# A hybrid encoder block on one Trainium2 core: two Strassen products with the low halves first, one load order for gate values and weights, a row of reciprocals, and another split of the last adds

## The chip, the cores and the metric

The kernel runs on one core of one Trainium2 chip. A core has five engines that each work through their own instruction list in order: PE (TensorE, matrix products), DVE (VectorE) and ACT (ScalarE) for elementwise work, POOL (GpSimd), and SP (SyncE), which here only issues transfers. They wait for each other by semaphores. The metric is the device time of one execution in microseconds (us); the kernel before takes 2518.39 us (median of 3 runs, 2517.55 to 2518.57).

## The reference, cut to what matters

One residual layer over 512 tokens of width 2048, in float32 (x, weights and output):

```
u  = RMSNorm(x)
q, k, v, conv_a, conv_b, gate_a, gate_b = split(u @ W_in)
y_A = neighbourhood_attention(q, k, v) @ W_attn_o          # 1024 -> 2048
y_B = silu(layer_norm(depthwise_conv(conv_a * sigmoid(conv_b)))) @ W_conv_o   # 1024 -> 2048
h  = x + RMSNorm((sigmoid(gate_a) * y_A + sigmoid(gate_b) * y_B) @ W_out)
u  = RMSNorm(h)
gate, up = split(u @ W_gate_up)                            # 2048 -> 2 x 5632
out = h + RMSNorm((silu(gate) * up) @ W_down)              # 5632 -> 2048
```

## The kernel before, in words

All activations are kept transposed: a tile has 128 channels by 512 tokens. Products are in a two-part form: each float32 operand is cast to a rounded "hi" (ACT, `whi_...`, `...h`) and a remainder "lo" (DVE, `wlo_...`, `...l`), and hi and lo products are added in PSUM. A function `gemm` (L168) does this for a chunk of weights of 128x1024: `wchunk` loads the raw chunk over SP's queue (L134; five buffers `raw`), casts hi on ACT (L135) and subtracts lo on DVE (L136), and for each of eight 128-blocks PE does three matmuls of 512 columns: hi weights by lo activations (L182), hi by hi (L185), lo by hi (L186).

**Strassen pairs.** Most of the two gate projections, of the feed-forward and of the down projection are done two output tiles at a time by a seven-product scheme, `strassen` (L237): 14 pairs g2 to g15, 39 pairs f5 to f43 and 16 pairs d0_0 to d1_14. The operands on the activation side hold hi in the first 256 columns and lo in the last 256. Each `product` (L275) is eight matmuls of 512 columns with the hi weights (L279) and then eight of 256 columns with the lo weights (L281), all into one PSUM tile. The seven are called in the order 11, T2, T1, T3, 21, 22, T4; in the first pair of a run of pairs ("apart": g2, f5, d0_0, d1_0) the 21 comes second. Between them DVE adds one PSUM tile into the next (L305, L310), ACT copies (L272, L287), and the hi and lo parts of the next weight sums are made (L245, L247).

**The merge.** `gated(i, j, ...)` (L724) makes output tile i of W_attn_o (j = 0) or W_conv_o (j = 1): it loads the stored gate value tile `gg` (`load_in_order`, that is a load on SP whose place in the program is kept), does the `gemm` into a PSUM tile `py`, and multiplies on DVE (L729). Sixteen tiles with j = 0 come first; the last operand tiles for them (`ya3` to `ya7`) are split inside the first of them, while three (`YA_EARLY`) are split earlier, in the last gate pair. At tiles 5, 6 and 7 a step of `layer_norm` (L685) is run: the mean by a matmul (`pmu`), eight subtractions (L698) and squares (ACT L381, added on DVE L384); then the column sums `rc_s` on PE (L339), `rc_v` on DVE (L347) and a power on POOL; then `rc_b` on PE (L356), eight multiplications (DVE L706), eight silu (ACT L708) and the hi/lo split `ych`, `ycl` (L713, L714). Then sixteen tiles with j = 1 follow; after each, POOL adds the j = 0 tile (L740) and the sum is split into `mh` on ACT and `ml` on DVE (L145) for W_out.

**Rows of the feed-forward.** The activations of W_down are scaled per token before, and unscaled after, by a row: `rstd` (L333) makes r = v^-1/2 by token with v the mean square, `by_column` (L352) spreads it by four transposing matmuls into a 128x512 row, which ACT copies to SBUF as `row[0]`, `row[1]`. `scaled` (L881, POOL L885) multiplies by it. Later the row is replaced by v * r, its reciprocal, by a second `by_column` and copy, at pair f39 (`ia0`) and between the two runs of d pairs (`ia1`); POOL multiplies results `ys` by it (L1020).

**The end.** The last norm gives `r_b`. Sixteen half tiles are then left in four groups `yg` of 128x1024: DVE multiplies each by the row (L1152); the first `G_ADD` = 2 groups are added to the output in memory by a transfer that accumulates (L1154, issued by POOL); for the others DVE adds the residual `hb` in two halves (L1157), and SP and ACT issue the output transfers (L1161).

**What sets the order.** The Python code is laid out once by a scheduler, which gives every engine a fixed list; `tc.keep_in_program_order` pins an instruction to its place in the program against the other pinned ones. Everything else can be put earlier or later than it is written. At run time each engine keeps to its list and waits where an operand is not there.

Of the kernel before, what the change touches and what calls it, by code (L numbers as in the profile page):

```python
# [25 lines left out]
F32 = mybir.dt.float32  # L26
# [5 lines left out]
P = 128  # L32
# [30 lines left out]
AHEAD = 6  # L63
LEFT, G_ADD = 4, 2
UN_EARLY, YA_EARLY = 2, 3
C_PRE, C_POST, C_FPRE, C_FPOST, C_LNG, C_LNB, C_BDW, C_WDW = 0, 16, 32, 48, 64, 72, 80, 88
# [4 lines left out]
def hybrid_block(ctx: ExitStack, tc, xT, vecs, rpb, mask, w_c0, w_qk, w_v, w_gg, w_cg, w_ao, w_co, w_out, w_g0, w_gu, w_dn, outT):  # L71
# [52 lines left out]

    def wchunk(src, name, parts=1, cast=nc.scalar.copy, raw=None):
        w = src.shape[-1]
        loaded = raw is not None
        raw = raw if loaded else wraw(name)[:, :w]
        hi = wp.tile([P, 1024], F32R, tag="whi", name=f"whi_{name}")[:, :w]
        lo = wp.tile([P, 1024], F32R, tag="wlo", name=f"wlo_{name}")[:, :w]  # L130
        for n in range(parts):
            s = slice(n * w // parts, (n + 1) * w // parts)
            if not loaded:
                nc.sync.dma_start(raw[:, s], src[:, s])  # L134
            cast(hi[:, s], raw[:, s])  # L135
            nc.vector.tensor_tensor(out=lo[:, s], in0=raw[:, s], in1=hi[:, s].bitcast(F32), op=ALU.subtract)  # L136
        taps(rate)
        return hi, lo
# [28 lines left out]

    def gemm(outs, acts, name, n=None, more=None, cols=slice(0, NT), between=(), pin=False, raw=None):  # L168

        n = n or len(acts)  # L170
        between = iter(between)
        for c in range(0, n, 8):
# [3 lines left out]
            for i, (ps, src) in enumerate(outs):  # L176
                hi, lo = wchunk(src[:, c * P : (c + w) * P], f"{name}_{i}_{c}", raw=None if c or i else raw)
                for k in range(w):
                    s = slice(k * P, (k + 1) * P)
                    ah, al = (t[:, cols] for t in acts[c + k])  # L180
                    first, last = c + k == 0, c + k == n - 1
                    mmul = nc.tensor.matmul(ps, hi[:, s], al, start=first, stop=False)  # L182
# [3 lines left out]
                    nc.tensor.matmul(ps, lo[:, s], ah, start=False, stop=last)  # L186
                next(between, lambda: None)()
# [67 lines left out]
    def strassen(w0, w1, op, name, n, s1=None, behind_last=None, first=None, quarters=None, apart=False):  # L255
# [18 lines left out]

        def product(ps, w, b, first=False, last=False):  # L275
            hi, lo = w if isinstance(w, tuple) else halved_weights(w, name)
            ws = [slice(k * P, (k + 1) * P) for k in range(HT)]
            for k, t in enumerate(op[b]):
                nc.tensor.matmul(ps, hi[:, ws[k]], t, start=first and k == 0, stop=False, skip_group_check=True)  # L279
            for k, t in enumerate(op[b]):  # L280
                nc.tensor.matmul(  # L281
                    ps[:, A], lo[:, ws[k]], t[:, A], start=False, stop=last and k == HT - 1, skip_group_check=True
                )

# [22 lines left out]
        s3 = wsum(a11, a21, ALU.subtract, 3)  # L307
        product(y, s3, "T3")
        p5 = copied(z, 3)
# [9 lines left out]
        c11 = done(x, 1)  # L319
        product(z, s4, "22", last=True)  # L320
        c12 = None if behind_last else done(z, 2)
# [9 lines left out]
    def rstd(acc, n, name, blocks=range(NB), pin=False, eps=None):  # L331
# [17 lines left out]
        nc.gpsimd.tensor_tensor(out=r[:, bs], in0=v[:, bs], in1=mhalf[:, bs], op=ALU.pow)  # L349
        return (r, v) if eps else r  # L350

# [372 lines left out]
    def gated(i, j, w, acts, more=None, raw=None):  # L724
        g = slot(f"gg{i}_{j}")
        load_in_order(g, g_d[j * KT + i])
        ps = bank(f"py{i}_{j}")
        gemm([(ps, w[i])], acts, f"y{i}_{j}", n=CT, more=more, raw=raw)
        nc.vector.tensor_tensor(out=g, in0=ps, in1=g, op=ALU.mult)  # L729
        return g  # L730
# [148 lines left out]
    y_d = dr.tile([2, KT, P, NT], F32, name="y_d")  # L879
    inverse = []  # L880

# [40 lines left out]
    for j in range(5, FT):  # L922
# [6 lines left out]
        for n, k0 in enumerate(DN_A):  # L929

            if j == k0 + KT + 1:
                ra, va = rstd([row[n]], KT * P, f"ra{n}", eps=TINY)
                ia = const.tile([P, NB], F32, name=f"ia{n}")
                nc.vector.tensor_tensor(out=ia, in0=va, in1=ra, op=ALU.mult)
                inverse.append(ia)
# [213 lines left out]
    for g, t in enumerate(yg):  # L1149

        out = hb[g] if g < G_ADD else t
        nc.vector.tensor_tensor(out=out, in0=t, in1=rb, op=ALU.mult)  # L1152
        if g < G_ADD:
            nc.gpsimd.dma_start(ov[4 * g : 4 * g + 4, :, B].rearrange("k p t -> p k t"), out, accum_op=ALU.add)  # L1154
            continue
        for m in range(0, 4, 2):
            nc.vector.tensor_tensor(  # L1157
                out=t[:, m : m + 2], in0=t[:, m : m + 2], in1=hb[g][:, m : m + 2], op=ALU.add
            )
# [87 lines left out]
```

## Time and profile before

| what | value |
|---|---|
| median of 3 runs | 2518.39 us (2517.55 to 2518.57) |
| the profiled execution | 2521.2 us, span 2519.4 us |
| granted TensorE clock over the span | 0.996 |
| PE busy | 2493.3 us, 99% of the span, 13399 instructions |
| DVE busy | 2007.7 us, 80% |
| ACT / POOL busy | 1193.5 us (47%) / 456.3 us (18%) |
| transfers | 456.60 MB, mean 181 GB/s |

The span is what lies between the first and the last instruction that the profiler recorded. In rows of the trace the first number is the start in us from the start of the span, the second the duration; "x8" groups eight instructions of one kind that follow each other, with the time from the first start to the last end. Matmuls are pipelined, so that the duration of one is longer than the distance to the next; distances between starts are what counts. What stands in brackets is the idle time of the engine ahead of the row, and what ended it. In windows, "PEclk" is the clock that the throttle granted to TensorE.

By stage: convolution, v and attention up to 500 us; gates 500 to 806; the merge j = 0 from 806 to 894 and j = 1 to 981; W_out to 1158; the feed-forward to 2051; W_down to 2500; the end.

### The profile page before, as it was taken

How to read it: one execution, taken by the hardware profiler on the slowest of the kernel's cores; microseconds unless marked ns; L12 is line 12 of the kernel's file. 1: busy time of each engine (PE TensorE's matmuls, PEld its weight loads, DVE VectorE, ACT ScalarE, POOL GpSimd, SP SyncE). 2: the span in 40 equal slices, each digit the busy share in tenths (PEclk: the TensorE clock that was granted, in tenths of full speed). 3: DMA queues.
4: the chain of work that ended last, by engine and by line, in shares of the span. 5: the costliest groups of instructions: out<-in, count | busy, mean ns of one | idle time of the engine just before them, and what ended most of it. 6: DMA issues, size and time to landing. Idle time of an engine off the chain costs nothing.

```text
span 2519.4 us, 35541 instructions
## 1 busy us (share of the span) xinstructions
PE 2493.3 (99%) x13399; PEld 2156.1 (86%) x13399; DVE 2007.7 (80%) x2566; ACT 1193.5 (47%) x1822; POOL 456.3 (18%) x489
## 2 busy tenths in 40 slices
PE   9999999999999999999999999999999999999997
PEld 7888888888888788889898888888888888888887
DVE  5999897597777555337898888899998889989886
ACT  5223333365555422225455555555555565556453
POOL 0110132220000011001101111122221203632352
PEclk9999999999999999999999999999999999999998
DMA  6246322386667535226455566566666678888886
GB/s 208 93 142 205 104 101 99 134 261 196 183 187 218 187 121 200 95 98 186 145 155 169 171 178 184 174 202 196 203 213 194 214 218 250 242 228 250 222 227 198
DMA packets 160300, 456.60 MB, mean 181 GB/s; under 512 B 17920, under 2 KB 30336, under 8 KB 160128
## 3 DMA queue, kind: packets, MB, share of 16 engines
q1 hardware_dynamic: 109984, 332.70, 38.4%
q0 software_dynamic: 30016, 86.53, 16.6%
q10 hardware_dynamic: 20128, 35.10, 3.7%
q8 instruction: 105, 1.72, 0.3%
q14 instruction: 67, 0.55, 0.1%
HBM read 384.53 MB, written 67.11 MB: 179 GB/s over the span
## 4 chain that ended last, share of the span: by engine, by line
PE 88%; DVE 7%; issue 2%; DMA 1%; ACT 1%; POOL 0%; SPq 0%; DVEq 0%; ACTq 0%; POOLq 0%
PE f L279 20%; PE f L281 10%; PE d L279 8%; PE g L279 7%; PE d L281 4%; PE pd L960 3%; PE g L281 3%; DVE cv L432 3%; PE qk L186 2%; PE qk L185 2%; PE qk L182 2%; PE po L185 2%; PE po L182 2%; PE po L186 2%; PE py L185 2%
## 5 line engine op out<-in xcount | busy, mean ns | idle before, releaser
L432 DVE SCALAR_TENSOR_TENSOR cv<-z,vec,cv 128x497 f32<-128x497 f32 (+14 forms) x240 | 190.9, 797 | 4.8
L136 DVE TENSOR_TENSOR wlo_wo<-raw_wo,whi_wo 128x1024 fp32r<-128x1024 f32 x36 | 47.5, 1319 | 106.6 <-ACT whi_wo L135 106.6
L862 POOL TENSOR_TENSOR row<-row,asq 128x512 f32<-128x512 f32 x30 | 40.3, 1343 | 413.3 <-ACT asq L861 413.3
L135 ACT CAST whi_wo<-raw_wo 128x1024 fp32r<-128x1024 f32 x36 | 37.8, 1050 | 130.0 <-PE po L185 122.7
L1020 POOL TENSOR_TENSOR ys<-ys,row 128x512 f32<-128x512 f32 x32 | 56.9, 1779 | 123.6 <-DVE ys L329 71.5
L135 ACT CAST whi_y<-raw_y 128x1024 fp32r<-128x1024 f32 x31 | 32.6, 1052 | 90.2 <-PE py L185 82.5
L729 DVE TENSOR_TENSOR gg<-py,gg 128x512 f32<-128x512 f32 x32 | 21.9, 690 | 63.7 <-PE py L186 60.3
L135 ACT CAST whi_qk<-raw_qk 128x1024 fp32r<-128x1024 f32 x32 | 33.6, 1051 | 77.1 <-PE qk L185 56.5
L136 DVE TENSOR_TENSOR wlo_qk<-raw_qk,whi_qk 128x1024 fp32r<-128x1024 f32 x32 | 40.2, 1257 | 32.4 <-ACT whi_qk L135 32.2
L885 POOL TENSOR_TENSOR an<-an,row 128x512 f32<-128x512 f32 x32 | 51.7, 1615 | 71.1 <-DMA an<-a_d 45.6
L136 DVE TENSOR_TENSOR wlo_y<-raw_y,whi_y 128x1024 fp32r<-128x1024 f32 x31 | 52.2, 1682 | 9.0 <-ACT whi_y L135 8.2
L349 POOL TENSOR_TENSOR r_r<-r_v,mhalf 128x2 f32<-128x2 f32 (+1 forms) x6 | 6.1, 1022 | 260.6 <-DVE r_v L347 208.3
L185 PE MATMUL py<-ych,whi_y 128*128 128x512 f32 x128 | 49.8, 389 | 0.0
L186 PE MATMUL py<-ych,wlo_y 128*128 128x512 f32 x128 | 49.8, 389 | 0.0
L182 PE MATMUL py<-ycl,whi_y 128*128 128x512 f32 x128 | 49.8, 389 | 0.0
L947 ACT ACTIVATE sg<-sg 128x512 f32<-128x512 f32 x39 | 24.7, 634 | 52.2 <-DVE sg L329 52.2
L513 POOL TENSOR_TENSOR bm<-braw,msk 128x128 f32<-128x128 f32 x56 | 42.6, 794 | 14.5 <-DMA braw<-in_rpb 14.4
L740 POOL TENSOR_TENSOR gg<-gg,gg 128x512 f32<-128x512 f32 x16 | 20.6, 1288 | 121.2 <-ACT whi_y L135 79.7
L440 POOL TENSOR_TENSOR csum<-csum,cv 128x512 f32<-128x512 f32 x7 | 12.7, 1818 | 144.4 <-DVE cv L432 144.4
L165 PE MATMUL f<-b,whi_f 128*128 128x256 f32 x128 | 36.3, 283 | 0.0
L166 PE MATMUL f<-b,wlo_f 128*128 128x256 f32 x128 | 36.3, 283 | 0.0
L164 PE MATMUL f<-b,whi_f 128*128 128x256 f32 x128 | 36.3, 283 | 0.0
(3200 smaller groups left out, 8734.5 us busy)
## 6 DMA issues: line engine op xcount, KB each, us to landing
raw_wo<-in_w_out SPq DMA_DIRECT2D x36, 512.0 KB, 3.6
raw_qk<-in_w_qk SPq DMA_DIRECT2D x32, 512.0 KB, 3.6
raw_w<-in_w_dn SPq DMA_DIRECT2D x24, 512.0 KB, 5.8
a_d<-sg ACTq DMA_DIRECT2D x44, 256.0 KB, 3.6
raw_v<-in_w_v SPq DMA_DIRECT2D x16, 512.0 KB, 4.4
gg<-g_d SPq DMA_DIRECT2D x32, 256.0 KB, 4.2
raw_y<-in_w_co SPq DMA_DIRECT2D x16, 512.0 KB, 3.5
raw_f<-in_w_g SPq DMA_DIRECT2D x16, 512.0 KB, 3.5
```

The costliest lines, as they stand in the source:

```text
L135: cast(hi[:, s], raw[:, s])
L136: nc.vector.tensor_tensor(out=lo[:, s], in0=raw[:, s], in1=hi[:, s].bitcast(F32), op=ALU.subtract)
L182: mmul = nc.tensor.matmul(ps, hi[:, s], al, start=first, stop=False)
L185: nc.tensor.matmul(ps, hi[:, s], ah, start=False, stop=False)
L186: nc.tensor.matmul(ps, lo[:, s], ah, start=False, stop=last)
L279: nc.tensor.matmul(ps, hi[:, ws[k]], t, start=first and k == 0, stop=False, skip_group_check=True)
L281: nc.tensor.matmul(ps[:, A], lo[:, ws[k]], t[:, A], start=False, stop=last and k == HT - 1, skip_group_check=True)
L432: nc.vector.scalar_tensor_tensor(out=a[:, to], in0=z[:, fr], scalar=col(C_WDW, i * CW + w), in1=a[:, to], op0=ALU.mult, op1=ALU.add)
L513: nc.gpsimd.tensor_tensor(out=bm[:, o + i - i0], in0=raw[:, :, i * BC : (i + 1) * BC], in1=msk[:, o + i - i0, None, :].broadcast_to([P, RO ...
L885: ins = nc.gpsimd.dma_start(t, a_d[DN_P + k]), nc.gpsimd.tensor_tensor(out=t, in0=t, in1=row[k // KT], op=ALU.mult)
L960: mmul = nc.tensor.matmul(ps, wt[:, s], t, start=k + i == 0, stop=k + i == DN_P + 1, skip_group_check=True)
L1020: tc.keep_in_program_order(nc.gpsimd.tensor_tensor(out=t, in0=t, in1=row[n], op=ALU.mult))
```

## The change

Four things are changed together.

1. In `product` a flag puts the eight lo matmuls (256 columns) ahead of the eight hi matmuls. It is set for T3 and for 22.
2. In `gated` the raw weights are loaded with `load_in_order` too, and the gate value's load stands behind the weights' in the program. `YA_EARLY` goes from 3 to 8, so that all eight `ya` tiles are split in the last gate pair.
3. The two replacements of `row` by v * r are done by a `reciprocal` of the 128x512 row in place on DVE; the second `by_column`, its copy and the small product v * r go.
4. `G_ADD` goes from 2 to 1: one group is added by the accumulating transfer, three by DVE. The DVE operations of this loop are pinned to the program's order.

```diff
-LEFT, G_ADD = 4, 2
-UN_EARLY, YA_EARLY = 2, 3
+LEFT, G_ADD = 4, 1
+UN_EARLY, YA_EARLY = 2, 8
...
-    def wchunk(src, name, parts=1, cast=nc.scalar.copy, raw=None):
+    def wchunk(src, name, parts=1, cast=nc.scalar.copy, raw=None, load=nc.sync.dma_start):
...
-                nc.sync.dma_start(raw[:, s], src[:, s])
+                load(raw[:, s], src[:, s])
...
-        def product(ps, w, b, first=False, last=False):
+        def product(ps, w, b, first=False, last=False, lo_first=False):
             hi, lo = w if isinstance(w, tuple) else halved_weights(w, name)
             ws = [slice(k * P, (k + 1) * P) for k in range(HT)]
-            for k, t in enumerate(op[b]):
-                nc.tensor.matmul(ps, hi[:, ws[k]], t, start=first and k == 0, stop=False, skip_group_check=True)
-            for k, t in enumerate(op[b]):
-                nc.tensor.matmul(
-                    ps[:, A], lo[:, ws[k]], t[:, A], start=False, stop=last and k == HT - 1, skip_group_check=True
-                )
+            steps = [(hi, slice(0, NT)), (lo, A)]
+            if lo_first:
+                steps.reverse()
+            for n, (wt, cols) in enumerate(steps):
+                for k, t in enumerate(op[b]):
+                    nc.tensor.matmul(
+                        ps[:, cols], wt[:, ws[k]], t[:, cols], start=first and n + k == 0,
+                        stop=last and n + k == HT, skip_group_check=True,
+                    )
...
-        product(y, s3, "T3")
+        product(y, s3, "T3", lo_first=True)
...
-        product(z, s4, "22", last=True)
+        product(z, s4, "22", last=True, lo_first=True)
...
     def gated(i, j, w, acts, more=None, raw=None):
         g = slot(f"gg{i}_{j}")
+        ps = bank(f"py{i}_{j}")
+        gemm([(ps, w[i])], acts, f"y{i}_{j}", n=CT, more=more, raw=raw, load=load_in_order)
         load_in_order(g, g_d[j * KT + i])
-        ps = bank(f"py{i}_{j}")
-        gemm([(ps, w[i])], acts, f"y{i}_{j}", n=CT, more=more, raw=raw)
         nc.vector.tensor_tensor(out=g, in0=ps, in1=g, op=ALU.mult)
...
-                nc.scalar.copy(row[0], by_column(inverse[0], "ia0"))
+                nc.vector.reciprocal(row[0], row[0])
...
-    nc.scalar.copy(row[1], by_column(inverse[1], "ia1"))
+    nc.vector.reciprocal(row[1], row[1])
...
-        nc.vector.tensor_tensor(out=out, in0=t, in1=rb, op=ALU.mult)
+        tc.keep_in_program_order(nc.vector.tensor_tensor(out=out, in0=t, in1=rb, op=ALU.mult))
```

The scheduler lays the lists out anew. In the changed kernel most lines stand three further down (L729 is now L732, L698 L701, L384 L387).

**DVE in the merge, j = 1.** `gg` rows are the multiplications that wait for the last matmul of their tile, `wlo` rows make the lo weights of a tile, `m...l` the split for W_out. Before, the list between the tiles 1 and 4:

```order
L729 TENSOR_TENSOR gg1_1_7826<-py1_1_7828,gg1_1_7826 128x512
L136 TENSOR_TENSOR wlo_y4_1_0_0_7948<-raw_y4_1_0_0_7946,whi_y4_1_0_0_7947 128x1024
L145 TENSOR_TENSOR m1l_7862<-gg1_1_7826,m1h_7861 128x512
L729 TENSOR_TENSOR gg2_1_7865<-py2_1_7867,gg2_1_7865 128x512
L136 TENSOR_TENSOR wlo_y5_1_0_0_7987<-raw_y5_1_0_0_7985,whi_y5_1_0_0_7986 128x1024
L145 TENSOR_TENSOR m2l_7901<-gg2_1_7865,m2h_7900 128x512
L729 TENSOR_TENSOR gg3_1_7904<-py3_1_7906,gg3_1_7904 128x512
```

And now, between the tiles 2 and 5:

```order
L732 TENSOR_TENSOR gg2_1_7865<-py2_1_7866,gg2_1_7865 128x512
L145 TENSOR_TENSOR m2l_7901<-gg2_1_7865,m2h_7900 128x512
L732 TENSOR_TENSOR gg3_1_7904<-py3_1_7905,gg3_1_7904 128x512
L136 TENSOR_TENSOR wlo_y4_1_0_0_7947<-raw_y4_1_0_0_7945,whi_y4_1_0_0_7946 128x1024
L145 TENSOR_TENSOR m3l_7940<-gg3_1_7904,m3h_7939 128x512
L136 TENSOR_TENSOR wlo_y5_1_0_0_7986<-raw_y5_1_0_0_7984,whi_y5_1_0_0_7985 128x1024
L732 TENSOR_TENSOR gg4_1_7943<-py4_1_7944,gg4_1_7943 128x512
```

The lo weights of tile 4 stood behind `gg1`, and stand behind `gg3` now. The pattern of four tiles' rows repeats: of the tiles 2 to 15 the seven even ones have their `wlo` behind the multiplication of the tile just before, the odd ones ahead of it.

**ACT and DVE at the layer norm, j = 0.** The numbered tiles are those of W_attn_o. On ACT, before, from the cast of the hi weights of tile 6 to the table load of silu:

```order
L135 CAST whi_y6_0_0_0_7396<-raw_y6_0_0_0_7395 128x1024
L135 CAST whi_y7_0_0_0_7485<-raw_y7_0_0_0_7484 128x1024
L695 ACTIVATE mu_7316<-pmu_7314 128x512
...
L381 ACTIVATE cv4_sq_7334<-cr4_7302 128x512
L135 CAST whi_y8_0_0_0_7519<-raw_y8_0_0_0_7518 128x1024
L381 ACTIVATE cv5_sq_7338<-cr5_7303 128x512
...
L135 CAST whi_y9_0_0_0_7553<-raw_y9_0_0_0_7552 128x1024
L704 COPY rc_bc_7426<-rc_b_7427 128x512
L708 ACT_TABLE_LOAD
```

Now; the eight silu (L711) and the eight casts `ych` (L716) follow the table load, and the hi weights of tile 8 follow the last of these:

```order
L698 ACTIVATE mu_7316<-pmu_7314 128x512
L384 ACTIVATE cv0_sq_7319<-cr0_7298 128x512
...
L384 ACTIVATE cv7_sq_7346<-cr7_7305 128x512
L135 CAST whi_y6_0_0_0_7395<-raw_y6_0_0_0_7394 128x1024
L135 CAST whi_y7_0_0_0_7484<-raw_y7_0_0_0_7483 128x1024
L707 COPY rc_bc_7426<-rc_b_7427 128x512
L711 ACT_TABLE_LOAD
```

The casts for tiles 6 and 7 moved behind the eight squares, those for 8 and 9 behind the whole chain of the norm. On DVE the list between `gg4` and the multiplications by the norm's row (L709) is now:

```order
L732 TENSOR_TENSOR gg4_0_7264<-py4_0_7265,gg4_0_7264 128x512
L701 TENSOR_TENSOR cr0_7298<-cr0_7298,mu_7316 128x512
...
L387 TENSOR_TENSOR cv0_sq_7319<-cv0_sq_7319,cv7_sq_7346 128x512
L350 TENSOR_SCALAR rc_v_7388<-rc_s_7383 128x4
L732 TENSOR_TENSOR gg5_0_7349<-py5_0_7350,gg5_0_7349 128x512
L136 TENSOR_TENSOR wlo_y6_0_0_0_7396<-raw_y6_0_0_0_7394,whi_y6_0_0_0_7395 128x1024
L136 TENSOR_TENSOR wlo_y7_0_0_0_7485<-raw_y7_0_0_0_7483,whi_y7_0_0_0_7484 128x1024
L732 TENSOR_TENSOR gg6_0_7392<-py6_0_7393,gg6_0_7392 128x512
```

Before, the lo weights of the tiles 6 and 7 stood ahead of the first subtraction, and those of tile 8 among the additions of squares. On PE `pmu` stands ahead of tile 5 in both. The sums `rc_s`, which stood behind the first three matmuls of tile 7, now stand right behind the 24 of tile 5; `rc_b`, which stood behind seven of tile 7, right behind the 24 of tile 6.

**DVE in pair d0_10, the second reciprocal.**

```order
L247 TENSOR_TENSOR d0_10l_19943<-d0_10q_19845,d0_10h_19941 128x1024
L1046 RECIPROCAL row1_10974<-row1_10974 128x512
L313 TENSOR_TENSOR d0_10_2_19837<-d0_10_2_19837,d0_10v2_19914 128x512
L319 TENSOR_TENSOR d0_10v3_19938<-d0_10_1_19836,d0_10v3_19938 128x512
L247 TENSOR_TENSOR d0_10l_19967<-d0_10s2_19869,d0_10h_19965 128x1024
```

It stands ahead of the addition that the product 22 of this pair waits for (L313, before L310), and itself waits for POOL's last multiplication by this row (L885). The first reciprocal (L941) stands in pair f37 between two casts.

More of the change, by code (lines that the diff above doesn't have):

```diff
@@ L166, in plain, with gemm @@
         nc.tensor.matmul(o, lo, t[:, A], start=False, stop=last, skip_group_check=True)
-    def gemm(outs, acts, name, n=None, more=None, cols=slice(0, NT), between=(), pin=False, raw=None):
+    def gemm(outs, acts, name, n=None, more=None, cols=slice(0, NT), between=(), pin=False, raw=None, load=nc.sync.dma_start):
         n = n or len(acts)
@@ L176, in gemm @@
             for i, (ps, src) in enumerate(outs):
-                hi, lo = wchunk(src[:, c * P : (c + w) * P], f"{name}_{i}_{c}", raw=None if c or i else raw)
+                hi, lo = wchunk(src[:, c * P : (c + w) * P], f"{name}_{i}_{c}", raw=None if c or i else raw, load=load)
                 for k in range(w):
@@ L349, in rstd @@
         nc.gpsimd.tensor_tensor(out=r[:, bs], in0=v[:, bs], in1=mhalf[:, bs], op=ALU.pow)
-        return (r, v) if eps else r
+        return r
     def by_column(r, name, blocks=range(NB), pin=False):
@@ L879, in hybrid_block @@
     y_d = dr.tile([2, KT, P, NT], F32, name="y_d")
-    inverse = []
     def scaled(k, pin=False):
@@ L931, in hybrid_block @@
             if j == k0 + KT + 1:
[L932 to L935, printed above, removed]
+                ra = rstd([row[n]], KT * P, f"ra{n}", eps=TINY)
             elif j == k0 + KT + 2:
@@ L1156, in hybrid_block @@
         for m in range(0, 4, 2):
-            nc.vector.tensor_tensor(
-                out=t[:, m : m + 2], in0=t[:, m : m + 2], in1=hb[g][:, m : m + 2], op=ALU.add
+            tc.keep_in_program_order(
+                nc.vector.tensor_tensor(
+                    out=t[:, m : m + 2], in0=t[:, m : m + 2], in1=hb[g][:, m : m + 2], op=ALU.add
+                )
             )
```

## The prediction

> **What bounds the kernel now.** I read the page first, then the table of what PE waited for, then windows of the stages that the change touches, and last the rows of each engine there.
>
> ```profile
> PE 2493.3 (99%) x13399; PEld 2156.1 (86%) x13399; DVE 2007.7 (80%) x2566; ACT 1193.5 (47%) x1822; POOL 456.3 (18%) x489
> ```
>
> PE is the bound nearly everywhere: only an edit that shortens PE's own work, ends one of its waits or makes a new one can move the time. Its longest waits are both in the merge:
>
> ```profile
> PE py L182 <- DVE gg L729: 2.1, 1, 2.1
> PE py L182 <- DVE ya4l L145: 1.9, 1, 1.9
> ...
> 872.00:875.00 3.00, 0.87 (x5) 0.43 (x4) 1.24 (x2) 1.04 (x1) 0.00 (x0) 1.00 1.00 339
> 875.00:879.00 4.00, 4.00 (x12) 3.11 (x11) 2.38 (x4) 0.00 (x0) 0.00 (x0) 0.57 1.03 380
> ```
>
> The windows' columns are us, busy time and count of PE, its weight loads, DVE, ACT and POOL, then PEclk. The wait of 2.1 us is followed by a stretch at clock 0.57: 12 matmuls in 4.00 us where full clock gives 17 or 18 (0.227 each, below), so some 1.4 to 1.6 us more. The wait of 1.9 us has no such stretch behind it.
>
> **Part 1, lo first.** What a turn from one width to the other costs is seen in starts:
>
> ```profile
> 1501.52 2.00 PE L279 MATMUL f<-t,f16h 128*128 128x512 f32 x8
> 1503.36 1.12 PE L281 MATMUL f<-t,f16l 128*128 128x256 f32 x8
> 1504.31 2.00 PE L279 MATMUL f<-t,f16h 128*128 128x512 f32 x8
> ...
> 903.72 0.69 DVE L729 TENSOR_TENSOR gg<-py,gg 128x512 f32<-128x512 f32 x1 [3.35 <-PE py L186]
> 909.16 0.69 DVE L729 TENSOR_TENSOR gg<-py,gg 128x512 f32<-128x512 f32 x1 [3.36 <-PE py L186]
> ...
> 1277.82 0.28 PE L164 MATMUL f<-b,whi_f 128*128 128x256 f32 x1
> 1278.18 0.28 PE L164 MATMUL f<-b,whi_f 128*128 128x256 f32 x1
> ```
>
> One product lasts 1504.31 - 1501.52 = 2.79 us. Without turns: 24 matmuls of 512 take 5.44 us between two `gg`, 0.2267 each; three of 256 (L164 to the next L164) take 0.36, 0.12 each; eight and eight make 2.774. A round of two turns thus costs 0.016 us. Lo first in T3 and 22 puts lo behind lo and hi behind hi: two rounds fewer in each of 65 pairs, and one in the four "apart" ones (22 then follows T3 directly), 134 rounds, **-2.2 us**. If the excess belongs to each new PSUM tile and not to the width, it is 0; if the rows' rounding hides 0.005, -2.8.
>
> The lo operand is needed 1.84 us (1503.36 - 1501.52) sooner. It is there:
>
> ```profile
> L279 PE MATMUL f<-b,f16h x24: 389/392/398, 1498.7 to 1514.3; 128*128 128x512 f32 x24
> L247 DVE TENSOR_TENSOR f16l<-f16s,f16h x4: 1224/1226/1226, 1496.3 to 1507.6; 128x1024 fp32r<-128x1024 f32 x4
> ```
>
> The last of the four sums' lo parts, that of 22, ends at 1507.6 + 1.23 = 1508.8; 22 is the sixth product and begins at 1498.7 + 5 x 2.79 = 1512.7. It would have to be 3.9 us later to be missed. I cost the advance at nothing.
>
> **Part 2, loads in one order.** It should remove the two waits above and the slow stretch: -1.9 - 2.1 - 1.5, and about 0.9 of small waits at the norm, which the new ones below replace: **-6.4** (0 to -7). On SP a gate value now follows its tile's weights; it is wanted 24 matmuls later than they are, so the swap costs nothing there. The eight `cr` tiles of 256 KB go ahead of tile 5's weights; at the 339 GB/s of the window 872 to 875 that is 6.2 us, which five raw buffers of one tile (5.4 us) each should cover. But the lists of DVE, ACT and PE have changed too. An engine does not pass a waiting instruction:
>
> ```profile
> 872.08 0.39 PE L186 MATMUL py<-ya7h,wlo_y 128*128 128x512 f32 x1
> 873.76 0.69 DVE L729 TENSOR_TENSOR gg<-py,gg 128x512 f32<-128x512 f32 x1 [3.41 <-DMA gg<-g_d]
> 874.37 1.22 DVE L136 TENSOR_TENSOR wlo_y<-raw_y,whi_y 128x1024 fp32r<-128x1024 f32 x1
> ...
> 835.73 0.40 PE L186 MATMUL py<-ya7h,wlo_y 128*128 128x512 f32 x1
> 835.97 0.59 PE L693 MATMUL pmu<-csum,ones 128*128 128x512 f32 x1
> 836.17 0.69 DVE L729 TENSOR_TENSOR gg<-py,gg 128x512 f32<-128x512 f32 x1 [3.36 <-PE py L186]
> ```
>
> `wlo_y`, which needs nothing of `gg`, starts when `gg` is through. *j = 1.* In seven even tiles `wlo` now stands directly behind the `gg` of the tile before. Let s be the start of that tile's last matmul. `gg` starts at s + 0.44 (835.73 to 836.17), `wlo` 0.61 later (873.76 to 874.37) and ends 1.23 after that, at s + 2.3. PE does the next tile's first two matmuls (L182, L185, hi weights) at s + 0.23 and s + 0.45 and wants the lo weights at s + 0.68. It waits 1.6 us; seven times that is **+11.2**. It is below the 1.9 that slowed nothing, so I add no slow clock. It could be more:
>
> ```profile
> 910.02 2.34 DVE L136 TENSOR_TENSOR wlo_y<-raw_y,whi_y 128x1024 fp32r<-128x1024 f32 x1 [0.17 <-ACT whi_y L135]
> ...
> 909.99 1.28 POOL L740 TENSOR_TENSOR gg<-gg,gg 128x512 f32<-128x512 f32 x1 [58.96 <-ACT whi_y L135]
> ```
>
> Beside POOL's addition, which began 0.03 us before it, `wlo` took 2.34 and not 1.23. In the new list `wlo` begins 0.61 behind `gg`, POOL 0.83 (909.16 to 909.99), so DVE is first by 0.2 and I keep 1.23; else the wait is 2.7 each, +7.8 in all, and slow clock may follow.
>
> *The norm, j = 0.* With T the start of `pmu` (835.97 here):
>
> ```profile
> 838.15 2.49 DVE L698 TENSOR_TENSOR cr<-cr,mu 128x512 f32<-128x512 f32 x4
> 845.97 1.22 DVE L136 TENSOR_TENSOR wlo_y<-raw_y,whi_y 128x1024 fp32r<-128x1024 f32 x1
> 847.11 1.49 DVE L384 TENSOR_TENSOR cv_sq<-cv_sq 128x512 f32<-128x512 f32 x2
> ...
> 848.65 0.49 PE L339 MATMUL rc_s<-ones,cv_sq 128*128 128x1 f32 x3
> ...
> 852.28 0.59 ACT L704 COPY rc_bc<-rc_b 128x512 f32<-128x512 f32 x1 [3.49 <-PE rc_b L356]
> 854.18 5.76 ACT L708 ACTIVATE cr<-cr,vec 128x512 f32<-128x512 f32 x8
> 859.84 0.60 ACT L713 CAST ych<-cr 128x512 fp32r<-128x512 f32 x1
> 862.77 2.18 ACT L713 CAST ych<-cr 128x512 fp32r<-128x512 f32 x4
> ```
>
> DVE's subtractions and additions took 838.15 to 848.60, 9.3 us without the `wlo` among them (1.14). Now they begin at about T + 1.25 (`pmu` 0.45, `mu` 0.60) and end at T + 10.55. PE reaches `rc_s` after tile 5, at T + 5.7: it waits **4.85**. Then `rc_v`, `gg5` and `wlo_y6` (0.1 + 0.6 + 1.2) stand on DVE ahead of tile 6's third matmul: **1.65**. Tile 6 and `rc_b` end at T + 19.5. ACT's `rc_bc` begins about then, its silu and casts need 7.56 (852.28 to 859.84) and 8 x 0.53, and `whi_y8`, another 0.95, is behind them: T + 32.4. PE has done tile 7 by T + 24.9: it waits **7.5** at tile 8, and about 1.0 more for `wlo_y8` behind `ycl` and `gg7`. Sum 15.0. The two long waits exceed the 2.1 us after which the trace shows clock 0.57, so each gets 1.5 more: **+18.0** (15 to 21). A page bears on that last term: the Trainium skill, "TensorE: Matmul & The Clock Gate", Part 1: The HAM clock gate, says that the clock halves after an idle window of about 3.4 us that runs free of the kernel. Here 2.13 us of idleness was enough, so the trace does not agree on the length; by the page alone the wait of 4.85 holds a whole window less than half the time, which as an estimate takes about 0.8 off.
>
> **Part 3, reciprocals.** Gone are two groups of transposes on PE:
>
> ```profile
> 1971.86 1.05 PE L356 MATMUL ia_b<-ident,ia 128*128 128x128 f32 x8
> 1972.67 2.10 PE L279 MATMUL f<-b,f40h 128*128 128x512 f32 x8
> ```
>
> 0.81 us and a first run that is 0.10 longer than the usual 2.00: **-1.8** for two. Added are two reciprocals of 128x512 on DVE. The trace has only narrow ones:
>
> ```profile
> L543 DVE RECIPROCAL st<-st 128x1 f32<-128x1 f32 x32 | 4.9, 156 | 0.5 <-ACT sc L542 0.2
> ...
> 2202.87 1.33 POOL L885 TENSOR_TENSOR an<-an,row 128x512 f32<-128x512 f32 x1
> 2202.97 0.69 DVE L310 TENSOR_TENSOR d<-d,d_10v 128x512 f32<-128x512 f32 x1
> 2206.22 2.00 PE L279 MATMUL d<-d,d_10h 128*128 128x512 f32 x8
> ```
>
> At the pace of other 128x512 operations one takes 0.69. The one in d0_10 waits for POOL until 2204.2, would end at 2204.9, and the addition for 22 at 2205.6, before PE wants it (2206.22): no loss. A divide that costs up to 9 ns an element more would not stand out in a row of 156 ns for one element, and makes 5.3 us for 512: then the addition ends at 2210.2 and PE waits 4.0, and some 0.8 in f37. Between 0 and +4.8 no row decides; I take the middle, **+2.4**. The Trainium skill, "VectorE: DVE Perf Modes", section "First, the fixed hardware budget", has the reciprocal as an iterative divide with a repeat count of 8; at the engine's 0.96 GHz ("Trainium Kernel Development and Optimization", NeuronCore Architecture) that would be 4.3 us for 512 elements as an estimate, and this term +3.4. No run here shows it.
>
> **Part 4, the end.** One group more on DVE:
>
> ```profile
> 2506.53 2.77 POOL L1154 DMA_DIRECT2D out<-hb  x2 [0.78 <-DVE hb L1152]
> 2509.87 2.49 DVE L1157 TENSOR_TENSOR yg<-yg,hb 128x512 f32<-128x512 f32 x4
> 2511.23 2.00 ACTq L1161 DMA_DIRECT2D out<-yg  x2
> ```
>
> Two additions of 0.6 put the last issue 1.2 us later; the second accumulating transfer, whose bytes lie ahead of the last outputs, is gone. The span ends at 2519.4, six us after the last issues (2511.23 + 2.00), so queued bytes matter: -2 to +1.2, taken **-1**.
>
> **The sum.** -2.2 - 6.4 + 11.2 + 18.0 - 1.8 + 2.4 - 1 = +20.2 on the profiled 2521.2 us; this lies 2.8 above the median, which I correct alike: 2518.4 + 20.2 = **2538.6**.
>
> **The rivals.**
> - *Dear waits* (0.17): in j = 1 POOL comes first and the seven waits are 2.7 us, long enough for slow clock as at 872 in some: +7.8 and up to 6 more, 2546 to 2553. For it: every `wlo` beside L740 in j = 1 has been slow. Against: POOL starts only 0.83 behind `gg`.
> - *Cheap norm* (0.15): ACT's and DVE's chains are shortened where both wait less for each other, without slow clock, and the reciprocals cost 0.69: -3 - 2.4 - 4, about 2529.
> - *Not slower* (0.08): the `wlo` and `whi` that the lists put late are not wanted late, because PE is itself behind at each of these tiles (weights landing late at 512 KB a tile hold it anyway). Then no new wait appears beside the old bound and parts 1 to 4 give -2.2 - 6.4 - 1.8 + 2.4 - 1 = -9.0, 2509.4. It decides from the point where less than 9 of the 29 us of new waits stay. Against it: the rows above show the j = 1 tiles 5.44 us apart, 24 matmuls at full pace, with no wait for a transfer.
> - *Lo first does nothing* (inside the others): +2.2.
>
> The likeliest, 0.60, is the sum with its own bounds, 2533 to 2544. Within 0.2% (5 us, about what a measurement of this kernel tells from no change) falls little of any case: 0.03. Faster by more 0.07, slower 0.90. The range that leaves out 2 in 10 goes down to half of the cheap norm and up into dear waits: 2526 to 2549.
>
> **What would show it.** Waits of PE at `rc_s` near 4.8 us and at tile 8 near 7.5, with clock near 0.6 behind both; seven waits of L186 on `wlo_y` of 1.6 us, 12.5 us apart; the waits on `ya4l` and `gg` gone; L279 and L281 groups of 16; a row RECIPROCAL 128x512 whose mean tells 0.7 from 4 or more, and PE's wait for L313 in d0_10. Wrong would be a merge that ends no later than before: then the lists do not set PE's pace.

## The result, and the profile after

The changed kernel takes 2550.91 us (median of 4 runs, 2550.28 to 2551.53) against 2518.48 us of the kernel before beside it: 1.0129 times as long, 95% interval 1.0112 to 1.0147. That is +32.4 us where +20.2 was forecast. The direction held; the time lies 1.9 us above the range. The profiled execution took 2551.37 us with a span of 2549.6, 30.2 more than the span before.

From the page of the changed kernel, busy time of the engines, and from the table of what PE waited for (us in total, times, longest):

```profile
PE 2497.4 (98%) x13383; PEld 2157.0 (85%) x13383; DVE 1989.3 (78%) x2568; ACT 1197.0 (47%) x1820; POOL 474.8 (19%) x488
...
PE py L186 <- DVE wlo_y L136: 12.0, 9, 1.5
PE py L182 <- ACT whi_y L135: 7.4, 1, 7.4
PE rc_s L342 <- DVE cv_sq L387: 4.7, 1, 4.7
PE d L283 <- DVE d_10l L247: 1.5, 1, 1.5
PE d L283 <- ACT d_2v L272: 1.5, 1, 1.5
...
PE d L283 <- ACT d_10v L272: 1.2, 1, 1.2
PE d L283 <- ACT d_6v L272: 1.2, 1, 1.2
```

The two old waits, on `ya4l` and `gg`, are gone. The first three rows are the ones forecast, in place and in size. The rows of the d pairs are not: of the five on the copies `v` (d_2 to d_10; three are shown) the prediction has nothing.

Where the time went, by stage: from the first matmul of a stage to the first of the next, read from the starts in both traces, in us.

| stage | before | after | difference |
|---|---|---|---|
| start to the first gate product | 482.6 | 482.2 | -0.4 |
| gates | 323.9 | 323.3 | -0.6 |
| merge | 184.0 | 211.35 | **+27.3** |
| W_out | 176.2 | 176.2 | 0.0 |
| feed-forward, from its norm on | 884.2 | 881.5 | -2.65 |
| d pairs, first run (d0), with the plain products ahead | 200.75 | 209.4 | **+8.6** |
| d pairs, second run (d1), with the plain products ahead | 200.05 | 199.65 | -0.4 |
| last plain products and last norm | 52.8 | 52.4 | -0.35 |
| end | 14.8 | 13.55 | -1.3 |

The first row shows the limit of such differences: no edit touches that stage, and over the fourteen profiles of this study it lay between 480.5 and 482.6. The last stage runs from the start of PE's last matmul to the end of the span. Read so, the merge of the kernel before ends at 990.6 and its tiles with j = 1 begin at 903.5; the 981 and 894 given ahead of the prediction are about 10 us early.

**The merge.** Rows of PE and DVE at tile 2 of j = 1, and POOL's addition there:

```profile
928.39 0.39 PE L185 MATMUL py<-ych,whi_y 128*128 128x512 f32 x1
930.25 0.50 PE L186 MATMUL py<-ych,wlo_y 128*128 128x512 f32 x1 [1.47 <-DVE wlo_y L136]
...
928.37 0.69 DVE L732 TENSOR_TENSOR gg<-py,gg 128x512 f32<-128x512 f32 x1 [1.94 <-PE py L186]
928.97 1.22 DVE L136 TENSOR_TENSOR wlo_y<-raw_y,whi_y 128x1024 fp32r<-128x1024 f32 x1
...
929.20 2.13 POOL L743 TENSOR_TENSOR gg<-gg,gg 128x512 f32<-128x512 f32 x1 [4.16 <-DVE gg L732]
```

The matmul with the lo weights starts 1.86 us behind the one ahead of it where the pace is 0.227, so 1.63 late, seven times: 11.4. DVE was first by 0.23 us and kept its 1.22; POOL paid, 2.13 in place of 1.28. At the norm PE waited 4.75 us at `rc_s`, behind tile 5, and 7.36 at tile 8:

```profile
838.85 0.39 PE L186 MATMUL py<-ya7h,wlo_y 128*128 128x512 f32 x1
843.98 1.86 PE L342 MATMUL rc_s<-ones,cv_sq 128*128 128x1 f32 x8 [4.75 <-DVE cv_sq L387]
...
869.38 0.79 PE L182 MATMUL py<-ya0l,whi_y 128*128 128x512 f32 x1 [7.36 <-ACT whi_y L135]
...
843.00:844.00 1.00, 0.02 (x1) 0.50 0.00 0
844.00:853.00 9.00, 8.08 (x22) 0.50 0.41 139
853.00:854.00 1.00, 1.00 (x5) 0.90 0.70 260
870.00:876.00 6.00, 5.13 (x13) 0.50 0.50 180
```

The last four are windows: us, PE's busy time and count, PEclk, the DMA share and GB/s. The clock stood at 0.50 from 843 to 853, through a third wait (1.3 us at `wlo_y6`), and from 870 to 876 at the least. Distances between starts above the usual ones, without the waits themselves, add to 3.8 us behind the first wait and 3.1 behind the second; 1.5 each had been set in.

The weights themselves were not late. By the landing times in the trace those of tile 6 were there at 822.1 and their cast to hi began at 842.3, those of tile 8 at 826.0 and 868.3, and those of the seven even tiles of j = 1 at least 25 us before their cast. The eight `cr` tiles of the norm were there at 818.8, 15.6 us ahead of DVE's first subtraction. What made PE wait was the place of the casts and the lo parts in the lists of ACT and DVE.

**The second reciprocal** and the row behind it:

```profile
L941 DVE RECIPROCAL row<-row x1: 3344/3344/3344, 1936.1 to 1936.1; 128x512 f32<-128x512 f32 x1
L1046 DVE RECIPROCAL row<-row x1: 3353/3353/3353, 2233.2 to 2233.2; 128x512 f32<-128x512 f32 x1
...
2236.48 0.67 DVE L313 TENSOR_TENSOR d<-d,d_10v 128x512 f32<-128x512 f32 x1
2237.66 1.21 DVE L247 TENSOR_TENSOR d_10l<-d_10s,d_10h 128x1024 fp32r<-128x1024 f32 x1
...
2238.93 1.21 PE L283 MATMUL d<-d,d_10l 128*128 128x256 f32 x8 [1.54 <-DVE d_10l L247]
```

It took 3.35 us (minimum, median and maximum of the one are given in ns), between the 0.69 and the 5.3 of the two bounds. PE then waits not for the addition L313 but for the lo operand of 22, which DVE makes still later and which, lo first, PE wants first.

### The profile page after: what moved, and what is told of

It is laid out like the page before. It is cut to its first block, busy times and chain, and to the rows that moved or that the text cites. A ratio compares the mean times of both kernels' runs of the same rounds, so it can differ in the third digit from the quotient of the medians.

```text
span 2549.6 us, 35381 instructions
## 1 busy us (share of the span) xinstructions
PE 2497.4 (98%) x13383; PEld 2157.0 (85%) x13383; DVE 1989.3 (78%) x2568; ACT 1197.0 (47%) x1820; POOL 474.8 (19%) x488
## 5 line engine op out<-in xcount | busy, mean ns | idle before, releaser
L865 POOL TENSOR_TENSOR row<-row,asq 128x512 f32<-128x512 f32 x30 | 53.6, 1786 | 394.6 <-ACT asq L864 394.6
L732 DVE TENSOR_TENSOR gg<-py,gg 128x512 f32<-128x512 f32 x32 | 22.1, 691 | 80.0 <-PE py L186 80.0
L743 POOL TENSOR_TENSOR gg<-gg,gg 128x512 f32<-128x512 f32 x16 | 27.5, 1721 | 146.5 <-DVE gg L732 146.5
L136 DVE TENSOR_TENSOR wlo_y<-raw_y,whi_y 128x1024 fp32r<-128x1024 f32 x31 | 37.6, 1223 | 4.8 <-ACT whi_y L135 4.6
L186 PEld LDWEIGHTS py<-ych,wlo_y 128*128 128x128 f32 x128 | 24.0, 188 | 18.1 <-DVE wlo_y L136 13.2
```

What stands on the lines that cost most here:

```text
L865: nc.gpsimd.tensor_tensor(out=row[n], in0=row[n], in1=sq, op=ALU.add)
```

## The experiments

Each edit is against the kernel before unless said otherwise. Stages are read as above.

### One part alone, or all but one

First lo first alone:

```diff
-        product(y, s3, "T3")
+        product(y, s3, "T3", lo_first=True)
...
-        product(z, s4, "22", last=True)
+        product(z, s4, "22", last=True, lo_first=True)
```

> Only lo first in T3 and 22; loads, reciprocals and the end as before. Theory A (lo first makes the five new waits of 1.4 us at T3 in the pairs d0_2 to d0_10: with 22 turned round, its output's second half is free only at the product's end, the work of DVE and POOL behind it comes later, and POOL's multiplication by the row falls on a weight sum of DVE): the waits are there without any other part, d0 about 7 us longer, gates and feed-forward 1.7 us shorter, in all about +5 us, 2523. Theory B (the waits come from the reciprocals or from the later start of the stage): no such wait, -2.2 us, 2516.

Measured: 2521.62 us against 2520.13, ratio 1.0008 (0.9998 to 1.0017). d0 is 7.3 us longer, with all five waits (1.2 us of idle time each in the profile, 1.5 at the first; with the slower restart each pair is about 1.4 longer); gates -0.35, feed-forward -1.7, d1 -0.3. So lo first makes the waits by itself, as theory A has it. The total came out smaller: +1.5 us against the kernel before beside it, where A had +5. The merge is 3.95 us shorter, which neither theory had: the scheduler laid the lists anew, `ya4l` came in time, and the wait for `gg` (2.0 us) was not followed by a slow clock.

Then the loads alone, with `YA_EARLY` 8:

```diff
-UN_EARLY, YA_EARLY = 2, 3
+UN_EARLY, YA_EARLY = 2, 8
...
-        load_in_order(g, g_d[j * KT + i])
         ps = bank(f"py{i}_{j}")
-        gemm([(ps, w[i])], acts, f"y{i}_{j}", n=CT, more=more, raw=raw)
+        gemm([(ps, w[i])], acts, f"y{i}_{j}", n=CT, more=more, raw=raw, load=load_in_order)
+        load_in_order(g, g_d[j * KT + i])
```

> Only the loads in one order and YA_EARLY 8; products, reciprocals and the end as before. Both theories: the merge is 27 us longer as in the changed kernel (waits of about 4.9, 1.3, 7.5, 1.3 and seven of 1.6 us, and half clock behind the first and third), 2545.5. A: no wait at T3 in d0. B (if the later start of the stage or another phase of the transfers is enough): the five waits of 1.4 are there, 2552.

Measured: 2546.5 us, ratio 1.0106 (1.0091 to 1.0121). The merge is 27.7 longer, with the same waits as in the changed kernel; d0 is as before (157.2 us for its pairs), without a wait. The whole loss of the merge is this part's; `YA_EARLY` 8 stands in the third experiment too, without it.

All but the loads (lo first, `YA_EARLY` 8, both reciprocals, `G_ADD` 1), against the changed kernel:

```diff
+        load_in_order(g, g_d[j * KT + i])
         ps = bank(f"py{i}_{j}")
-        gemm([(ps, w[i])], acts, f"y{i}_{j}", n=CT, more=more, raw=raw, load=load_in_order)
-        load_in_order(g, g_d[j * KT + i])
+        gemm([(ps, w[i])], acts, f"y{i}_{j}", n=CT, more=more, raw=raw)
```

> The change without the loads in one order (YA_EARLY 8 kept). The merge keeps its old order: no wait at rc_s, tile 8 or on wlo_y in j = 1; the wait on ya4l is gone (-1.9), that on gg stays. Gates -0.6, feed-forward -2.6, the end -1.3 as in the changed kernel. A and B both have the waits in d0 (+8.5): about +1.5 us, 2520. If d0's waits hang on the merge, they are gone and it is 2512.

Measured: 2520.04 us, ratio 1.0003 (0.9994 to 1.0013): no change. The merge is 4.05 shorter, d0 7.1 longer, feed-forward -2.6, the end -1.4. d0 has four of the five waits at T3 and the one at the second reciprocal, so they do not hang on the merge.

All but lo first (loads, `YA_EARLY` 8, reciprocals, `G_ADD` 1), against the changed kernel:

```diff
-        product(y, s3, "T3", lo_first=True)
+        product(y, s3, "T3")
...
-        product(z, s4, "22", last=True, lo_first=True)
+        product(z, s4, "22", last=True)
```

> The change without lo first. The merge +27.3, the transposes -1.8, the end -1.3, the wait at the second reciprocal 1.4 to 1.7. A: no waits of 1.4 at T3 in d0, in all +26, 2544. B: the five waits stay, 2551.

Measured: 2549.08 us against 2520.13, ratio 1.0116 (1.0101 to 1.0131). No wait of 1.4 at T3 in the pairs d0_2 to d0_10, as A says. The 29.0 us over the kernel before lie between A's 26 and B's 33, since the reciprocal costs more than expected: d0 is 3.05 longer. From its waits and rows:

```profile
PE d L279 <- DVE d L310: 1.9, 1, 1.9
...
PE d L279 <- ACT d_12v L272: 1.4, 1, 1.4
...
2229.47 3.35 DVE L1043 RECIPROCAL row<-row 128x512 f32<-128x512 f32 x1 [3.43 <-POOL an L884]
2232.74 0.67 DVE L310 TENSOR_TENSOR d<-d,d_10v 128x512 f32<-128x512 f32 x1
```

DVE stood still 3.43 us for POOL's last multiplication by the row, then divided for 3.35, and was still behind one pair later, where PE waited a second time. These were 3.6 us of delayed starts (2.0 and 1.6) against 0.6 that the transposes saved there.

### What in lo first makes the waits in d0

Lo first in T3 alone:

```diff
-        product(y, s3, "T3")
+        product(y, s3, "T3", lo_first=True)
```

> Lo first in T3 alone. Theory A (22's turn moves POOL's multiplication onto the weight sum): no wait of 1.4 at T3 in d0, d0 at 157 us or a little less; 69 rounds of turns saved, -1.1 us, 2517.3. Rival A2 (T3's own turn makes the waits): d0 about 164.5.

Measured: 2516.52 us, one execution, beside 2519.09 of the kernel before; the d0 pairs take 157.05, no wait. And in 22 alone:

```diff
-        product(z, s4, "22", last=True)
+        product(z, s4, "22", last=True, lo_first=True)
```

> Lo first in 22 alone. Theory A: the waits of 1.4 at T3 in d0 are there, d0 about 164 to 165 us, +6 in all. A2: none, d0 157, -1.1 us in all.

Measured: 2518.96 us beside 2519.09; the d0 pairs take 162.95 (before 157.2), with four waits of 1.4 (d_4 to d_10; that of d_2 is not there). It is 22's turn.

What it does is seen in one pair. In the kernel before, DVE's weight sum for the next pair (L267), POOL's scaling (L885), DVE's addition of p1 and ACT's copy, which T3 waits for:

```profile
2152.39 2.13 POOL L1020 TENSOR_TENSOR ys<-ys,row 128x512 f32<-128x512 f32 x1 [5.42 <-PE d L279]
2155.41 0.87 POOL L885 DMA_DIRECT2D an<-a_d  x1
2160.95 1.89 POOL L885 TENSOR_TENSOR an<-an,row 128x512 f32<-128x512 f32 x1 [1.93 <-DMA an<-a_d]
...
2158.72 1.23 DVE L267 TENSOR_TENSOR d_8s<-d_8s,d_8q 128x1024 f32<-128x1024 f32 x1
2159.86 0.69 DVE L305 TENSOR_TENSOR d<-d,d_6v 128x512 f32<-128x512 f32 x1
...
2160.59 0.59 ACT L272 COPY d_6v<-d 128x512 f32<-128x512 f32 x1 [1.56 <-DVE d L305]
```

and with lo first alone (the first experiment), the same pair:

```profile
2148.06 1.29 POOL L1023 TENSOR_TENSOR ys<-ys,row 128x512 f32<-128x512 f32 x1 [6.14 <-DVE ys L332]
2150.26 0.87 POOL L888 DMA_DIRECT2D an<-a_d  x1
2155.42 1.67 POOL L888 TENSOR_TENSOR an<-an,row 128x512 f32<-128x512 f32 x1
...
2155.42 2.76 DVE L267 TENSOR_TENSOR d_8s<-d_8s,d_8q 128x1024 f32<-128x1024 f32 x1
2158.10 0.69 DVE L308 TENSOR_TENSOR d<-d,d_6v 128x512 f32<-128x512 f32 x1
...
2158.82 0.59 ACT L272 COPY d_6v<-d 128x512 f32<-128x512 f32 x1 [3.23 <-DVE d L308]
...
2159.46 1.21 PE L283 MATMUL d<-d,d_6l 128*128 128x256 f32 x8 [1.22 <-ACT d_6v L272]
```

Before, POOL had to wait for its tile's load and multiplied 2.2 us behind the start of the sum, when the sum was done. Now the load is issued earlier (5.2 us ahead of the sum and not 3.3), the tile is there, and multiplication and sum start in the same instant: the sum takes 2.76 us and not 1.23, and the addition, the copy and T3 follow 1.4 late. Theory A had the direction wrong (POOL's work comes earlier, not later) and the collision right. The first row of each list shows one step of the way there: counted from the pair's first matmul (2153.15 and 2149.71), POOL's multiplication of a result tile `ys` begins 0.9 us sooner and takes 1.29 and not 2.13, and the load behind it is issued 1.7 sooner. Why 22's turn gives such lists was not tried.

To take the collision away, the multiplication was left out, with lo first in both products, and its transfers kept:

```diff
-        ins = nc.gpsimd.dma_start(t, a_d[DN_P + k]), nc.gpsimd.tensor_tensor(out=t, in0=t, in1=row[k // KT], op=ALU.mult)
+        ins = [nc.gpsimd.dma_start(t, a_d[DN_P + k])]
+        if k < FT - DN_A[0] - KT - 2:
+            ins.append(nc.gpsimd.tensor_tensor(out=t, in0=t, in1=row[k // KT], op=ALU.mult))
```

> Lo first in both, as in the first experiment, but POOL's multiplication by the row (an) is left out for the tiles scaled inside the d0 pairs, while their transfers stay; so these tiles go unscaled into the second part of the down projection. If this multiplication beside DVE's weight sum is what makes the sum 2.8 us and PE wait (theory A), the sum is back at about 1.2 us and the five waits are gone: d0 at 157 us. If the order of DVE's list alone or the transfers make them, they stay: d0 164.5.

Measured: 2515.1 us beside 2519.09, one execution each; d0's pairs 157.1, no wait. The group of that sum (both of its kind, one in each run of pairs; minimum, median and maximum in ns), with lo first and then without the scaling:

```profile
L267 DVE TENSOR_TENSOR d_8s<-d_8s,d_8q x2: 1225/1993/2761, 2155.4 to 2360.4; 128x1024 f32<-128x1024 f32 x2
```

```profile
L267 DVE TENSOR_TENSOR d_8s<-d_8s,d_8q x2: 1225/1226/1227, 2153.2 to 2353.7; 128x1024 f32<-128x1024 f32 x2
```

So the multiplication beside the sum is the cause. Without it lo first is worth what the turns promise, 2.2 us over gates, feed-forward and d pairs; the merge gives the other 3.9 of that profile. One pair of the third experiment shows the same from the other side. There the sum begins 0.17 us ahead of POOL, keeps its 1.23, and T3 does not wait:

```profile
2112.52 1.23 DVE L267 TENSOR_TENSOR d_4s<-d_4s,d_4q 128x1024 f32<-128x1024 f32 x1
2112.69 2.21 POOL L887 TENSOR_TENSOR an<-an,row 128x512 f32<-128x512 f32 x1
```

The Trainium skill, "SBUF — State Buffer", section "SBUF: two separate sides", has the rule: a GpSimd operation that reads SBUF and a VectorE operation with two SBUF inputs share a pair of ports as a lock that the first holds to its end. The rows agree: 2.76 is the sum's 1.23 and 1.53 more, about one multiplication of POOL alone (1.33), and in the merge the one that came 0.23 us late paid.

### The price of the divide

Part 3 alone, with a copy in each reciprocal's place:

```diff
-                nc.scalar.copy(row[0], by_column(inverse[0], "ia0"))
+                nc.vector.tensor_copy(row[0], row[0])
...
-    nc.scalar.copy(row[1], by_column(inverse[1], "ia1"))
+    nc.vector.tensor_copy(row[1], row[1])
```

> The kernel before with part 3 alone, and in it a copy of the row onto itself in the place of each reciprocal, so that results are multiplied by the row and not by its reciprocal. Theory C (the divide's 3.35 us in d0_10 make the wait): the copy takes about 0.7 or less, no wait, d0 shorter than before by the transposes, 156.3, and the feed-forward by 0.9. Theory D (the place in DVE's list behind POOL makes it): waits of 1.4 and more stay, d0 159 to 160.

Measured: 2517.46 us beside 2519.09. The copies took 0.41 and 0.43 us. Feed-forward -1.2; d0's pairs 157.16, with no wait but one of 0.3, in a pair whose sum took 2.50 us beside POOL. The saving of the transposes does not show there, but the waits of 2.0 and 1.6 are gone, though DVE still stood still 3.41 us for POOL ahead of the copy. They are the divide's, theory C.

### Whether DVE's list makes the merge's waits

The loads as in the second experiment, and in j = 1 the order on DVE written out:

```diff
+        nc.scalar.copy(hi, raw)
+        tc.keep_in_program_order(nc.vector.tensor_tensor(out=lo, in0=raw, in1=hi.bitcast(F32), op=ALU.subtract))
+        ahead.append((hi, lo, g))
...
+        while len(ahead) < min(KT, i + 3):
+            next_weights()
...
+        tc.keep_in_program_order(nc.vector.tensor_tensor(out=g, in0=ps, in1=g, op=ALU.mult))
```

> The loads of the second experiment (one order, YA_EARLY 8), and in j = 1 alone the weights' lo parts and the gg multiplications are pinned on DVE in the order gg(i), then wlo of tile i + 3; nothing else. If the seven waits of 1.6 us come from DVE's list (wlo directly behind the gg of the tile before), they go and the norm's waits stay: 11 us less than there, 2535. If they come from the loads' own order (weights landing late), they stay: 2546.

Measured: 2534.89 us (two runs), ratio 1.0058 (1.0040 to 1.0077). Its waits of PE:

```profile
PE py L182 <- ACT whi_y L135: 7.3, 1, 7.3
PE rc_s L339 <- DVE cv_sq L384: 4.8, 1, 4.8
PE py L186 <- DVE wlo_y L136: 1.8, 2, 0.9
```

The seven are gone (12.0 in nine became 1.8 in two, both at the norm), the norm's stay. The merge is 11.7 shorter than with the loads alone.

Then the same in j = 0 too, one loop over both:

```diff
+    for n in range(2 * KT):
+        i, j = n % KT, n // KT
+        while len(ahead) < min(2 * KT, n + 3):
+            next_weights()
+        if j == 0 and LN_AT <= i < LN_AT + 3:
+            next(norm)
```

> The same pinning in j = 0 too, so that the layer norm's work on DVE is laid around the weights and not ahead of them; the weights of a tile are asked for three tiles ahead. If the lists alone make the waits at rc_s, tile 6 and tile 8, with the slow clock behind them, all go: the merge at 178 to 181 us (184 before), 2512 to 2516. If the layer norm's loads ahead of the weights on SP are the cause, waits at tiles 6 to 8 stay and it is over 2525.

Measured: 2514.1 us in the profiled execution, against 2519.93. A second execution took 8124.14 us; its cause is not known, and what follows rests on the first. The longest wait of PE in the merge is now

```profile
PE py L765 <- DVE wlo_y L747: 0.7, 1, 0.7
```

and the merge takes 177.8 us against 184.0 before. The loads in one order cost nothing here; the lists that the scheduler laid around them did. In j = 0 this edit also puts loads of weights ahead of the norm's, so it doesn't part the two by itself there. The landing times given under the merge do: the weights of the tiles 6 and 8 had been there for 20 us and more.

### What the parts are worth together

Lo first except in the d0 pairs, the first reciprocal alone, `G_ADD` 1; the loads and `YA_EARLY` as before:

```diff
-LEFT, G_ADD = 4, 2
+LEFT, G_ADD = 4, 1
...
+        turned = not name.startswith("d0")
...
-        product(y, s3, "T3")
+        product(y, s3, "T3", lo_first=turned)
...
-        product(z, s4, "22", last=True)
+        product(z, s4, "22", last=True, lo_first=turned)
...
-                nc.scalar.copy(row[0], by_column(inverse[0], "ia0"))
+                nc.vector.reciprocal(row[0], row[0])
```

> The parts that gained, loads as before: lo first in T3 and 22 except in the d0 pairs, only the first reciprocal (in f37), one accumulated group at the end. By the stages of the earlier runs: gates -0.4, merge -3.9, feed-forward -2.6, d0 0, d1 -0.3, the end -1.3: 8.5 us faster than before, ratio 0.9966. If the gain of the merge is only the phase of that profile (no slow clock behind the wait for gg) it is half of that, ratio 0.998.

Measured: 2510.82 us (five runs) against 2519.93, ratio 0.9964 (0.9951 to 0.9976). Merge -3.9, feed-forward -2.7, d0 0.0, d1 -0.3, the end -1.5.

The same with the loads and the pinned list of the tenth experiment:

```diff
-UN_EARLY, YA_EARLY = 2, 3
+UN_EARLY, YA_EARLY = 2, 8
...
+    for n in range(2 * KT):
...
+        tc.keep_in_program_order(nc.vector.tensor_tensor(out=g, in0=ps, in1=g, op=ALU.mult))
```

> The same with the loads in one order and DVE pinned as in the tenth. The wait for gg (2.1 us) goes too and 1.5 us may come at the merge's first tile: 1 to 3 us faster than the run before, ratio to the kernel before about 0.996. If the pinned lists cost elsewhere, it is slower than that run.

Measured: 2510.0 us, ratio 0.9957 (0.9944 to 0.9971). The merge is 2.65 us shorter than in the run before it, but the two intervals overlap: that it beats that run is not shown, that both beat the kernel before is.

## Why the prediction was right or wrong

| step | forecast | measured | read from |
|---|---|---|---|
| lo first, fewer turns (measured without d0) | -2.2 | -2.4 | first experiment: gates -0.35, feed-forward -1.74, d1 -0.3 |
| the advance of the lo operand and what 22's turn moves | 0 | **+7.3** | d0 in the first experiment |
| old waits of the merge gone | -6.4 | -6.0 | 2.1 + 2.3 of delayed starts and 1.6 of slow clock in the trace before; +27.3 less the next three rows is the same |
| seven waits in j = 1 | +11.2 | +11.4 | 7 x 1.63 |
| waits at the norm | +15.0 | +15.0 | 4.9 + 1.3 + 7.5 + 1.3 of delayed starts |
| slow clock behind two of them | +3.0 | **+6.9** | 3.8 + 3.1 |
| reciprocals and transposes | +0.6 | +1.9 | fourth experiment: -1.2 and +3.05 |
| the end | -1.0 | -1.3 | the changed kernel's last stage |

The measured column adds to 32.8; the spans differ by 30.2. The rest is that the last waits of d0 fall together (8.6 there, not 7.3 + 3.05) and the 0.8 by which untouched stages differ (-0.4 and -0.35 in the table of stages).

**The step that failed** is the one that ended with "I cost the advance at nothing"; it cost 7.3 us, all in the first run of d pairs. It looked at a pair of the feed-forward, at the lo operand of 22 alone, and took its 3.9 us of slack for all 69 pairs. In the d0 pairs POOL scales tiles beside DVE, and there another order shifts POOL's multiplication onto a weight sum. By the profile the last thing that T3 waited for was the copy behind that sum, and not its lo operand. The profile of before had both halves: the rows in which `wlo` took 2.34 us beside POOL were quoted in the prediction, for the merge, and the page's group of L885 says that this multiplication was held by its load (of 71.1 us that POOL was idle ahead of the 32 of them, 45.6 ended with a load):

```profile
L885 POOL TENSOR_TENSOR an<-an,row 128x512 f32<-128x512 f32 x32 | 51.7, 1615 | 71.1 <-DMA an<-a_d 45.6
```

What hid the collision was a load that came late. The rival *dear waits* names this cost in the wrong place: its time, 2546 to 2553, holds the result, its mechanism was not at work in j = 1, where POOL paid.

**The slow clock** was right in place and mis-sized: 1.5 us for each wait came from a stretch of 3.4 us behind a wait of 2.1; behind waits of 4.75 and 7.36 the clock stayed at 0.50 for about 10 and at least 6 us. Without the 3.9 us by which this term was too small, or without the 7.3 of the step above, the time would have come inside the range.

**The merge's waits** were right to a few tenths, from the lists of the engines and durations of single rows. The ninth and tenth experiments and the landing times show the cause: with DVE's list written out the waits go while the loads stay in one order, and the weights had landed long before they were cast.

**The reciprocal** came between the bounds (3.35 us). The estimate of 4.3 from the Trainium skill, "VectorE: DVE Perf Modes", section "First, the fixed hardware budget", was a quarter too long and nearer than the row of 0.69. The step's own mistake was smaller: it looked for PE's wait at one product and not at the backlog behind it.

`YA_EARLY` and `G_ADD` were not run by themselves. That `YA_EARLY` 8 adds nothing is likely: with lo first the wait on `ya4l` is gone at 3 (first and eleventh experiment) as at 8 (third).

## What to carry to other kernels

Where a scheduler lays out the engines' lists, an edit that only names an order for some transfers can move work that no line of it touches: read the new lists of each engine, and for each operand of the bound engine what now stands ahead of it. A slack found in one stage is not the slack of another in which a further engine is at work; ask of each stage which transfer's lateness keeps two engines apart. And the parts of a change are worth running apart: each of the four had something to gain here, the loads only once DVE's list was written out, and two lost it again at one place, the d0 pairs.

## What was not expected of the hardware

The same wait of PE for `gg`, 1.9 to 2.1 us, was followed by a slow clock in two of eight profiles and not in the others. Windows of PE in the kernel with the copies (eighth experiment) and in the one with lo first alone:

```profile
868.00:872.00 4.00, 2.38 (x11) 1.00 0.90 311
872.00:876.00 4.00, 3.58 (x11) 0.68 1.02 386
```

```profile
868.00:872.00 4.00, 1.99 (x10) 1.00 0.98 358
872.00:876.00 4.00, 4.00 (x19) 1.00 1.04 397
```

It isn't the length alone: 2.04 us was followed by a slow clock in the eighth experiment and by none in the fifth. It may be where the wait falls, which would fit what the Trainium skill, "TensorE: Matmul & The Clock Gate", Part 1: The HAM clock gate, says of a window that runs free of the kernel, though the idle window of about 3.4 us that it gives is longer than this wait. The two profiles with the slow clock are also the only two of the eight that still have the wait on `ya4l`, some 60 us earlier. No run here moved a wait on purpose to part the two. About 1.6 us of the 3.9 by which the merge got shorter in six of the experiments are this alone.

A reciprocal of 128x512 takes 3.35 us, 6.5 ns an element, while one of 128x1 takes 156 ns and shows nothing of it.
